# A hybrid decoder layer: projections in groups of 256 columns with one 512-column product for both parts of the moving operand

## The chip, the cores and the metric

The kernel runs on one core of a Trainium2 chip. The metric is the device time of one execution in microseconds (us), the median of several runs. TensorE (PE) multiplies: a weight load (LDWEIGHTS) brings in a stationary operand of up to 128 columns, and a product (MATMUL) streams a moving operand of up to 512 columns past it and adds the result in PSUM. VectorE (DVE), ScalarE (ACT) and GpSimd (POOL) do the elementwise work. Transfers are issued from the queue of SyncE (SP) in the main. Each engine executes its own instructions in program order, and semaphores order the engines among each other.

## What is computed

One decoder layer for 256 positions of width 2048 in float32: a normalisation, one large projection, two groups of attention heads, an output projection, and a mixture of 32 experts with two experts for each position. Cut to what matters:

```python
xn = rms_norm(h, attn_norm_w[layer])
proj = xn @ w_in[layer]                       # (256, 2048) @ (2048, 5696)
(nq, kcmp, vcmp, kslc, vslc, kwin, vwin, ngate, fq, fk, fv, ff) = jnp.split(proj, split_at, axis=-1)
o_nsa = nsa_mixer(...)                        # 16 heads, from the first eight
o_fox = fox_mixer(...)                        # 16 heads, from the last four
mixed = jnp.concatenate([rms_norm(o_nsa, nsa_out_norm_w[layer]),
                         rms_norm(o_fox, fox_out_norm_w[layer])], axis=-1)
h = h + mixed @ w_out[layer]
h = h + hier_moe(rms_norm(h, ffn_norm_w[layer]), ...)
return rms_norm(h, final_norm_w)
```

The change touches `xn @ w_in` alone. Its 64 columns for gates and forget logits are computed apart from the rest; 5632 columns remain.

## The kernel before

The projections are made with split operands. Every float32 matrix is written as a rounded part `hi` and a rest `lo`, both in a reduced float32 format, and a product of two such matrices is the sum of three products: hi with hi, hi with lo, lo with hi. They are added in the same place in PSUM.

x is transposed once at the start (`x_chunk`, L280): for each of 16 steps of depth (128 rows of the depth each) TensorE transposes two tiles, ScalarE writes the rounded part `xh(k)` and VectorE the rest `xl(k)`. They lie in four tiles `x0` to `x3` (L242): two for the rounded parts and two for the rests, eight steps each.

The weights are a stream of items (`items`, L161). An item is a tile of 1 MB, 512 rows by 512 columns, in one of three buffers `r0` to `r2` (`stream_dma`, L164). It is issued three items ahead. Each item is split in two halves by `stream_conv` (L179): ScalarE rounds 128x1024 elements, VectorE subtracts; the result goes to one of three buffers `c0` to `c2`, tiles named `cv_`. The split of a half is issued two halves ahead, and so waits until TensorE has read the half before the present one.

`project` (L306) makes four items for 512 columns, four steps of depth in each. A step (`chunk`) issues 12 products of 256 columns. For queries and keys ("T") the weights are stationary, in blocks of 128 columns, and x is the moving operand (`t_mm`, L289). For values ("N", half of the columns of a "TN" projection) x is stationary and the weights move (`n_mm`, L297). Each has its own weight load. The sums of a projection fill two PSUM banks, and four banks are there, so the next projection can run while the last is read out. There are 11 projections and 44 items: compressed keys and values (`kcv`), the keys and values of the two other branches (`kvs`, `kvw`), two of queries (`q`), and for the second head group two of queries (`fq`) and four of keys with values (`fkv`), where the two column ranges of 256 are loaded by two transfers.

After the last item of a projection `post` scales the sums by the row factors, straight out of PSUM: `row_scale` (L331) on VectorE, and for values a ScalarE scaling for each of two row tiles.

The first projection is written out on its own (L1036 to L1064), with the transposes and the sums of squares (`square`, L256) of x between its steps. From the second on, `run_items` (L225) issues after each step one step of `background`, four to an item: a stage of the attention of one pair of heads, and one step of the smaller work queued in `misc` and `splits`. Attention units are queued by `post` of the projection that completes their operands.

Behind the projections come the output projection (`out_block`, L884, tiles `wo`), 16 items whose products have 512 columns, with its operand split by `split_o` into the buffers `x0` to `x3` as these come free (`o_split`, L867); then the router; then 16 pairs of experts, whose weights come through a ring of buffers (`SLOTS`, L33) in a fixed order, each transfer issued when its buffer is released.

## Time and profile before

| | |
|---|---|
| median of 3 runs | 1419.55 us (1418.47 to 1419.59) |
| the profiled execution | 1417.83 us |
| its span | 1416.1 us |
| TensorE busy | 1310.2 us, 7462 products |
| VectorE, ScalarE busy | 496.6 us, 316.3 us |
| transfers | 480.02 MB |

The profile comes from one execution. Its page gives the busy time of each engine and its course over 40 slices; views of the trace give tables of stretches, the waits, the chain of work that ended last, and the instructions in order of time. Matmul durations in it overlap: one product is shown with some 280 ns where the next begins 120 ns later, so rates are read from the start of a run of products to its end, over their count.

### The profile page before, as it was taken

Reading aid. Unit: us, or ns where it says so; the run is one execution under the profiler, and the core shown is the slowest. Engines: PE = TensorE matmul, PEld = TensorE weight load, DVE = VectorE, ACT = ScalarE, POOL = GpSimd, SP = SyncE. Lnnn points to the kernel's source line nnn. Section 1 sums busy time; section 2 is a strip of 40 time slices with the busy share of each in tenths; the row PEclk is TensorE's granted clock in tenths of the full one; section 3 lists DMA queues with packets and bytes.
Section 4 is the critical chain, followed back from the end, with each engine's and each line's share of the span. In section 5 each row is a group of like instructions: output and inputs, shape, how many; then the busy total and the mean of one; then the engine's idle time right before and its main releaser. Section 6 shows DMA issues by size and latency. Waiting matters only on the chain.

```text
span 1416.1 us, 18174 instructions
## 1 busy us (share of the span) xinstructions
PE 1310.2 (93%) x7462; PEld 769.4 (54%) x7462; DVE 496.6 (35%) x990; ACT 316.3 (22%) x632; POOL 79.7 (6%) x95
## 2 busy tenths in 40 slices
PE   9999999999998999999988997997998899799885
PEld 8999899998787534334324333442433344243332
DVE  4656777767766204113103021220310212031022
ACT  5445555545544000000000000000010000000003
POOL 0300010221101003000000000000000000000003
PEclk9999999999999999999999999999999999999998
DMA  8654344654696899999999999999999999999994
GB/s 276 210 165 158 125 144 151 221 164 164 240 341 223 344 414 405 417 421 421 421 420 421 421 421 421 420 421 421 421 421 421 420 421 421 420 420 421 421 401 158
DMA packets 116697, 480.02 MB, mean 339 GB/s; under 512 B 14368, under 2 KB 40832, under 8 KB 68352
## 3 DMA queue, kind: packets, MB, share of 16 engines
q1 hardware_dynamic: 112240, 474.53, 84.6%
q10 hardware_dynamic: 4368, 4.27, 0.9%
q8 instruction: 60, 0.98, 0.3%
q14 instruction: 29, 0.24, 0.0%
HBM read 476.63 MB, written 2.14 MB: 338 GB/s over the span
## 4 chain that ended last, share of the span: by engine, by line
PE 50%; DMA 42%; DVE 4%; ACT 2%; issue 1%; POOL 0%; SPq 0%; DVEq 0%; ACTq 0%; POOLq 0%
DMA e_u<-in_expert_w_up_dram 16%; DMA e_d<-in_expert_w_down_dram 16%; DMA e_g<-in_expert_w_gate_dram 11%; PE bu L114 7%; PE fkv_ps L114 6%; PE wo L114 6%; PE bg L114 5%; PE by L114 5%; PE fq_ps L114 3%; PE bx L114 2%; PE q_ps L114 2%; PE bo L114 2%; PE kcv_ps L114 2%; PE kvw_ps L114 2%; PE kvs_ps L114 2%; PE o L114 2%
## 5 line engine op out<-in xcount | busy, mean ns | idle before, releaser
L114 PE MATMUL by<-e_d,hids 128*64 128x512 f32 (+2 forms) x1072 | 234.1, 576 | 32.3 <-DMA e_d<-in_expert_w_down_dram 31.7
L114 PE MATMUL bu<-e_u,xg 128*64 128x512 f32 x1024 | 242.5, 597 | 9.5 <-DMA e_u<-in_expert_w_up_dram 9.5
L114 PE MATMUL bg<-e_g,xg 128*64 128x512 f32 x1024 | 236.6, 596 | 12.5 <-DMA e_g<-in_expert_w_gate_dram 12.5
L1330 DVE TENSOR_TENSOR ys<-by,ys 128x512 fp32r<-128x512 f32 x60 | 40.0, 688 | 455.4 <-ACT ys L1329 454.3
L114 PEld LDWEIGHTS by<-e_d,hids 128*64 128x64 f32 x1072 | 78.4, 137 | 180.9 <-issue 121.2
L114 PEld LDWEIGHTS bg<-e_g,xg 128*64 128x64 f32 x1024 | 80.7, 137 | 145.7 <-issue 111.1
L114 PEld LDWEIGHTS bu<-e_u,xg 128*64 128x64 f32 x1024 | 78.6, 136 | 143.5 <-issue 114.3
L1344 DVE TENSOR_TENSOR y<-y,bo 128x512 f32<-128x512 f32 x112 | 72.0, 684 | 151.0 <-PE bo L114 151.0
L1329 ACT CAST ys<-by 128x512 fp32r<-128x512 f32 x60 | 35.2, 586 | 310.9 <-PE by L114 197.2
L114 PE MATMUL bo<-ys,scT 128*128 128x512 f32 x240 | 73.5, 427 | 13.3 <-DVE y L1344 5.8
L114 PE MATMUL wo<-cv_wo,ohi 128*128 128x512 f32 x256 | 80.6, 396 | 0.0
L114 PEld LDWEIGHTS bx<-s,hh 128*128 128x128 f32 x512 | 64.1, 193 | 23.7 <-issue 13.0
L114 PE MATMUL bx<-s,hh 128*128 128x256 f32 x512 | 70.4, 291 | 4.6 <-DVE y L1344 2.9
L114 PEld LDWEIGHTS bo<-ys,scT 128*128 128x128 f32 x240 | 38.0, 188 | 60.1 <-issue 45.1
L1258 DVE TENSOR_TENSOR xg<-bx,fw 128x512 f32<-128x512 f32 x64 | 43.6, 690 | 77.1 <-PE bx L114 77.1
L114 PE MATMUL fkv_ps<-xhl,cv_fkv 128*128 128x256 f32 x384 | 58.5, 288 | 0.0
L1452 POOL TENSOR_TENSOR o<-y,e_fnw 128x256 f32<-128x256 f32 (+2 forms) x12 | 10.1, 866 | 835.9 <-DVE y L1365 835.9
L114 PE MATMUL fkv_ps<-cv_fkv,xhl 128*128 128x256 f32 x384 | 56.4, 283 | 0.0
L114 PEld LDWEIGHTS wo<-cv_wo,ohi 128*128 128x128 f32 x256 | 46.9, 188 | 10.4 <-issue 1.2
L188 DVE TENSOR_TENSOR cv_fkv<-raw_fkv,cv_fkv 128x1024 fp32r<-128x1024 f32 x32 | 43.3, 1352 | 24.9 <-ACT cv_fkv L187 24.7
L114 PE MATMUL fq_ps<-xhl,cv_fq 128*128 128x256 f32 x384 | 51.6, 287 | 0.0
L114 PEld LDWEIGHTS fkv_ps<-xhl,cv_fkv 128*128 128x128 f32 x384 | 50.8, 191 | 1.3 <-issue 0.5
(288 smaller groups left out, 1397.3 us busy)
## 6 DMA issues: line engine op xcount, KB each, us to landing
e_g<-in_expert_w_gate_dram SPq DMA_DIRECT2D x128, 1024.0 KB, 19.8
e_u<-in_expert_w_up_dram SPq DMA_DIRECT2D x128, 1024.0 KB, 19.8
e_d<-in_expert_w_down_dram SPq DMA_DIRECT2D x124, 1024.0 KB, 19.8
raw_fkv<-in_w_in_dram SPq DMA_DIRECT2D x32, 512.0 KB, 4.5
raw_wo<-in_w_out_dram SPq DMA_DIRECT2D x16, 1024.0 KB, 5.5
raw_q<-in_w_in_dram SPq DMA_DIRECT2D x8, 1024.0 KB, 5.1
raw_fq<-in_w_in_dram SPq DMA_DIRECT2D x8, 1024.0 KB, 4.9
raw_kvs<-in_w_in_dram SPq DMA_DIRECT2D x4, 1024.0 KB, 6.9
```

The source lines that it names most:

```text
L114: pe.matmul(o, l, r, start=start, stop=stop, skip_group_check=True)
L188: dve.tensor_tensor(lo, r, hi.bitcast(F32), ALU.subtract)
L1258: dve.tensor_tensor(xt_[:, i0:i0 + per, 0:m], bx.rearrange("p (i s) -> p i s", i=per), fw[:, 4 * j + i0:4 * j + i0 + per].unsqueeze(2).bro ...
L1329: act.copy(hi, by[n])
L1330: dve.tensor_tensor(lo, by[n], hi.bitcast(F32), ALU.subtract)
L1344: dve.tensor_tensor(y[t][:, ns], base[t][:, ns], bo, ALU.add)
L1452: (dve if last else pool).tensor_tensor(o[t][:, ns], y[t][:, ns], fnw[:, ns], ALU.mult)
```

## The change

A projection is now 256 columns over the whole depth: two items of 1024 rows by 256 columns, with eight steps in each, and 22 projections of either kind "T" or "N". The two parts of an operand lie next to each other: `xb(k)` is `xh(k)` and `xl(k)` in 512 columns, and a split half of weights has `hi` and `lo` of a step side by side. One product of 512 columns multiplies the rounded stationary part with both parts of the moving operand at once; its result fills a whole bank, the product with hi in one half, that with lo in the other. A second product of 256 columns adds the stationary rest. At the end ScalarE copies one half out of PSUM, VectorE adds the other, and `post` reads the sum in SBUF. Half of the queries and of the compressed keys and values is so handed on two items earlier. Four background steps remain in each item. The x buffers change their order, and with them the ring. The first split of all is made in two parts.

```diff
-    psb = ps_st.enter_context(tc.tile_pool(name="psb", bufs=4, space=PSUM))
+    psb = ps_st.enter_context(tc.tile_pool(name="psb", bufs=2, space=PSUM))
...
+    def banks(name):
+        return psb.tile([P, 2, 512], F32, tag="b", name=name)
...
     def stream_conv(h):
...
-        cv = big.tile([P, 2, 2, 512], F32R, tag=f"c{h % 3}", name=f"cv_{nm}_{hf}")
-        hi, lo = cv[:, 0], cv[:, 1]
-        r = raws[i][:, 2 * hf:2 * hf + 2, :]
-        act.activation(hi, r, AF.Copy)
-        dve.tensor_tensor(lo, r, hi.bitcast(F32), ALU.subtract)
+        n2 = nk // 2
+        cv = big.tile([P, n2, 2, 2048 // nk], F32R, tag=f"c{h % 3}", name=f"cv_{nm}_{hf}")
+        hi, lo = cv[:, :, 0, :], cv[:, :, 1, :]
+        r = raws[i][:, n2 * hf:n2 * hf + n2, :]
+        n = n2 if h else n2 // 2
+        for k in range(0, n2, n):
+            act.activation(hi[:, k:k + n], r[:, k:k + n], AF.Copy)
+            dve.tensor_tensor(lo[:, k:k + n], r[:, k:k + n], hi[:, k:k + n].bitcast(F32), ALU.subtract)
...
-    xhl = [big.tile([P, 8, T], F32R, tag=f"x{i}", name=f"xhl{i}") for i in range(4)]
+    xhl = [big.tile([P, 4, 2, T], F32R, tag=f"x{i}", name=f"xhl{i}") for i in range(4)]
+
+    def xb(k):
+        return xhl[k // 4][:, k % 4].rearrange("p a t -> p (a t)")
...
-        mm(ps, hi[:, cs], xh(k), st, False)
-        mm(ps, hi[:, cs], xl(k), False, False)
-        mm(ps, lo[:, cs], xh(k), False, k == 15)
...
-        mm(ps, xh(k)[:, tk], hi[:, cs], st, False)
-        mm(ps, xh(k)[:, tk], lo[:, cs], False, False)
-        mm(ps, xl(k)[:, tk], hi[:, cs], False, k == 15)
...
+    def project(col, kind, name, post):
...
+        def chunk(kg, kk, hi, lo, both):
+            k = kg * 8 + kk
+            if not b:
+                b.append(banks(f"{name}_ps"))
+            for c in range(2):
+                cs = slice(c * P, c * P + P)
+                if kind == "T":
+                    mm(b[0][:, c, :], hi[:, cs], xb(k), k == 0, False)
+                    mm(b[0][:, c, 0:T], lo[:, cs], xh(k), False, k == 15)
+                else:
+                    mm(b[0][:, c, :], xh(k)[:, cs], both, k == 0, False)
+                    mm(b[0][:, c, 0:T], xl(k)[:, cs], hi, False, k == 15)
+
+        def end():
+            t_ = wk.tile([P, 2, T], F32, tag="sum", name=f"{name}_sum")
+            act.copy(t_, b[0][:, :, T:])
+            dve.tensor_tensor(t_, b[0][:, :, 0:T], t_, ALU.add)
+            post(t_)
+
+        for kg in range(2):
+            items.append((f"{name}{kg}", w_in[kg * 1024:(kg + 1) * 1024, col:col + 256], 8,
+                          lambda kk, hi, lo, both, kg=kg: chunk(kg, kk, hi, lo, both), end if kg == 1 else None))
...
-    project(C_KC, "T", "kcv", post_kcv)
-    project(C_KS, "TN", "kvs", lambda b: post_kv(b, 0))
-    project(C_KW, "TN", "kvw", lambda b: post_kv(b, 1))
+    for i in range(2):
+        project(C_KC + 256 * i, "T", f"kcv{i}", lambda s_, i=i: post_kcv(s_, i))
+    for br, col in enumerate((C_KS, C_KW)):
+        project(col + 256, "N", f"v{br}", lambda s_, br=br: post_v(s_, br))
+        project(col, "T", f"k{br}", lambda s_, br=br: post_k(s_, br))
...
+            project(C_FK + c, "T", f"fk{G}{hf}", kept.append)
+            project(C_FV + c, "N", f"fv{G}{hf}", lambda s_, G=G, hf=hf: post_fv(s_, G, hf))
...
-    for i in range(4):
-        _, _, chunk, post, _ = items[i]
+    for i in range(2):
+        post = items[i][4]
...
-        if i == n_proj - 3:
+        if i == n_proj - 2:
             o_split(0)
-            for q in range(8):
-                misc.append(split_later(q))
+            for q in range(0, 8, 2):
+                misc.append(split_later(q, q + 1))
             rs_o(0)
```

## Rows read from the trace of the kernel before

**Rows 1.** The page, parts 1 and 2: busy time; busy tenths in 40 slices.

```profile
PE 1310.2 (93%) x7462; PEld 769.4 (54%) x7462; DVE 496.6 (35%) x990; ACT 316.3 (22%) x632; POOL 79.7 (6%) x95
...
PE   9999999999998999999988997997998899799885
...
DMA  8654344654696899999999999999999999999994
```

**Rows 2.** Table of stretches: length, busy us by engine (instructions), clock, DMA share, GB/s.

```profile
37.77:99.40 61.63, 61.63 (x534) 58.99 (x533) 35.81 (x56) 25.39 (x32) 11.91 (x16) 1.00 0.55 174
99.40:157.50 58.10, 55.60 (x457) 53.85 (x456) 39.07 (x98) 32.81 (x66) 0.61 (x1) 1.00 0.50 163
157.50:194.60 37.10, 35.18 (x290) 33.16 (x289) 28.25 (x87) 22.18 (x54) 3.10 (x5) 1.00 0.40 129
194.60:259.70 65.10, 65.10 (x538) 61.83 (x538) 47.68 (x144) 36.66 (x94) 9.69 (x12) 1.00 0.50 151
259.70:348.40 88.70, 87.83 (x734) 82.64 (x734) 61.83 (x140) 45.30 (x98) 20.83 (x20) 1.00 0.56 185
348.40:447.70 99.30, 99.13 (x476) 79.23 (x475) 67.68 (x104) 50.17 (x78) 4.64 (x6) 1.00 0.69 254
520.00:600.00 80.00, 76.54 (x382) 31.89 (x380) 22.21 (x30) 6.84 (x14) 12.10 (x8) 1.00 1.00 412
```

**Rows 3.** TensorE's waits to 460 us: us in total, times, longest.

```profile
PE bpt L741 <- DVE st_n L641: 2.8, 2, 1.9
...
PE csc L114 <- DVE st_n L641: 1.0, 1, 1.0
PE o L114 <- DVE pT_f L607: 0.9, 1, 0.9
...
PE s_n L114 <- DVE q L695: 0.5, 1, 0.5
...
PE t_f L604 <- DVE st_f L588: 0.2, 1, 0.2
```

**Rows 4.** The same waits in the expert part, 520 to 1380 us.

```profile
PE by L114 <- DMA e_d<-in_expert_w_down_dram: 31.7, 24, 1.3
PE bg L114 <- DMA e_g<-in_expert_w_gate_dram: 12.5, 10, 1.3
PE bu L114 <- DMA e_u<-in_expert_w_up_dram: 9.5, 9, 1.3
```

**Rows 5.** The chain of work in order of time: start, us, what, count.

```profile
51.15 1.37 PE bgt L114 x12
...
99.41 20.17 PE q_ps L114 x168
...
376.80 35.49 PE wo L114 x156
...
575.40 13.73 PE by L114 x64
```

**Rows 6.** The page, part 5: busy us, mean ns of one, then idle before.

```profile
L1344 DVE TENSOR_TENSOR y<-y,bo 128x512 f32<-128x512 f32 x112 | 72.0, 684 | 151.0 <-PE bo L114 151.0
L1329 ACT CAST ys<-by 128x512 fp32r<-128x512 f32 x60 | 35.2, 586 | 310.9 <-PE by L114 197.2
```

**Rows 7.** Instructions in order of time at a projection's end: start, us, what [idle before].

```profile
318.26 0.68 DVE L336 TENSOR_TENSOR fox_m<-fkv_ps,rsb 128x512 f32<-128x512 f32 x1
...
318.91 0.84 ACT L797 ACTIVATE fox_m<-fkv_ps,rsx 128x256 f32<-128x256 f32 x2 [1.82 <-PE fkv_ps L114]
...
319.64 1.06 ACT L187 ACTIVATE cv_fkv<-raw_fkv 128x1024 fp32r<-128x1024 f32 x1
...
320.73 1.23 DVE L188 TENSOR_TENSOR cv_fkv<-raw_fkv,cv_fkv 128x1024 fp32r<-128x1024 f32 x1 [1.78 <-ACT cv_fkv L187]
```

**Rows 8.** The start: ScalarE and VectorE in order of time; last, a piece of the chain.

```profile
10.55 0.48 DVE L285 SCALAR_TENSOR_TENSOR xhl<-xt,vec,xhl 128x256 fp32r<-128x256 f32 x1
13.57 1.06 ACT L187 ACTIVATE cv_kcv<-raw_kcv 128x1024 fp32r<-128x1024 f32 x1 [1.28 <-DMA raw_kcv<-in_w_in_dram]
...
20.86 1.05 ACT L258 ACTIVATE oraw<-xs 128x1024 f32<-128x1024 f32 x1
21.80 0.19 ACT L258 ACTIVATION_READ_ACCUMULATOR oraw<-xs 128x1 f32 x1
22.14 0.47 ACT L284 ACTIVATE xhl<-xt,vec 128x256 fp32r<-128x256 f32 x1
...
32.02 5.76 PE kcv_ps L114 x48
```

**Rows 9.** Transfers: two groups of issues, one issue, and the gates' weights landing.

```profile
raw_fkv<-in_w_in_dram SPq DMA_DIRECT2D x32, 512.0 KB, 4.5
...
raw_q<-in_w_in_dram SPq DMA_DIRECT2D x8, 1024.0 KB, 5.1
...
14.65 7.43 SPq L376 DMA_DIRECT2D gmem<-in_w_in_dram  x1
...
DMA to landing us min/median/max: 2.9/7.3/10.7
```

More of the change, by code (lines that the diff above doesn't have):

```diff
@@ L226, in run_items @@
         for i in range(lo_i, hi_i):
-            _, _, chunk, post, _ = items[i]
+            nk, post = items[i][2], items[i][4]
             stream_dma(i + DMA_AHEAD)
-            for kk in range(4):
-                h = 2 * i + kk // 2
-                if kk % 2 == 0:
-                    stream_conv(h + 2)
-                hi, lo = halves[h]
-                chunk(kk, hi[:, kk % 2, :], lo[:, kk % 2, :])
-                background()
+            for kk in range(nk):
+                if kk % (nk // 2) == 0:
+                    stream_conv(2 * i + 2 + 2 * kk // nk)
+                run_chunk(i, kk)
+                if (kk + 1) % (nk // 4) == 0:
+                    background()
             if post is not None:
@@ L886, in out_block, with chunk @@
         ns = slice(n * 512, (n + 1) * 512)
-        def chunk(kg, kk, hi, lo):
+        def chunk(kg, kk, hi, lo, _):
             if not b:
-                b.extend(bank(f"wo{part}{n}{t}") for t in range(2))
+                bb = banks(f"wo{part}{n}")
+                b.extend(bb[:, t, :] for t in range(2))
             k = part * 8 + kg * 4 + kk
@@ L912, in out_block @@
             r0 = part * 1024 + kg * 512
[L913 to L914 removed]
+            items.append((f"wo{part}{n}{kg}", w_out[r0:r0 + 512, ns], 4,
+                          lambda kk, hi, lo, both, kg=kg: chunk(kg, kk, hi, lo, both), post if kg == 1 else None))
     for part in range(2):
@@ L1034, in tile_kernel @@
     stream_dma(2)
-    for i in range(4):
-        _, _, chunk, post, _ = items[i]
+    for i in range(2):
+        post = items[i][4]
         if i:
             stream_dma(i + DMA_AHEAD)
-        for kk in range(4):
-            k = 4 * i + kk
+        for kk in range(8):
+            k = 8 * i + kk
             if k == 0:
```

166 lines of the change are left out of this document (74 added, 92 removed).

## The prediction

> **What bounds the kernel now.** I read the page first, then the stretches, then what TensorE waits for, then the chain. The page shows TensorE busy for most of the span and the DMA engines full only from about the 17th of 40 slices on [rows 1]. The table of stretches cuts the first third: in the projections (up to 348.4 us) and the output projection (to 447.7 us) the PE column is nearly the whole length of each stretch, VectorE stands at 58% to 76%, ScalarE at 41% to 60% and the DMA share at 0.40 to 0.69; from 520 us on the DMA share is 1.00 [rows 2]. So the front part is bound by TensorE's instruction stream and the expert part by transfers. TensorE's waits in the projection part after the first 40 us come to 2.8 + 1.0 + 0.9 + 0.5 + 0.2 = 5.4 us, all on VectorE [rows 3]. In the expert part it waits for expert weights, 31.7 + 12.5 + 9.5 us [rows 4]. That transfer stream has a fixed number of bytes behind a start that the program places after the output projection: what the front part gains or loses moves the end by as much.
>
> **What a product costs.** Where nothing else interrupts, 168 products of 256 columns take 20.17 us, 120.1 ns each, and 156 of 512 columns take 35.49 us, 227.5 ns each [rows 5]. The granted clock of these stretches is 1.00 in the table [rows 2], the 2.4 GHz level, at which 256 and 512 columns last 106.7 and 213.3 ns: each product thus shows some 13 to 14 ns over its columns, whatever its length. Both rows have a new 128-column stationary operand for each product.
>
> **The change, part by part.**
>
> *Products.* 5632 columns are projected (the gates' 64 go another way): 44 blocks of 128 by 16 steps of depth, 704 groups. (For the values, two blocks of 128 rows by 22 blocks of 256 columns: 704 as well.) Each group now has three 256-column products, 2112 in all; it will have one of 512 and one of 256. Three cost 3 x 120.1 = 360.3 ns, the pair 227.5 + 120.1 = 347.6 ns: 12.7 ns less, and 704 x 12.7 ns = 8.9 us. The columns are the same, 768: what goes is one fixed part per group, not a third of the work. No stretch of before has 512 and 256 in turn. From below the pair could cost 360 ns (the 512-column product pays the fixed part twice), which saves nothing. From above the nearest rows have 64-column weights: 64 products of 512 columns in 13.73 us (214.5 ns) and 12 of 256 in 1.37 us (114.2 ns) [rows 5], a pair of 328.7 ns, so 31.6 ns and 22 us saved. I take 12.7 ns: the two rows with 128-column weights are the nearest, and they agree on the fixed part.
>
> The Trainium skill, "TensorE: Matmul & The Clock Gate", section "Back-to-back issue gap", gives the isolated warm gap as N/2.4 + 2.5 ns, as an estimate 109.2 and 215.8 ns here, and speaks against most of this gain: a group would save 2.5 ns and all of them 1.8 us. The trace disagrees with its size: the measured 120.1 and 227.5 ns have a fixed part five times as large.
>
> *The halves' sum.* Each of the 22 new projections of 256 columns ends with a ScalarE copy of 128x512 out of PSUM and a VectorE addition of the same size, then the old scaling. By the nearest rows these take 0.586 us (L1329) and 0.684 us (L1344) [rows 6], 12.9 us on ScalarE and 15.0 us on VectorE. Neither engine sets the end in a mean: in the busiest stretch VectorE has 28.25 of 37.1 us [rows 2], and one addition in two items (some 16 us there) brings 76% to 80%. What can hurt is the order on ScalarE. The copy waits for the last product, and the split of the next weights (`stream_conv`, ScalarE then VectorE, 1.06 + 1.23 us) is queued behind it; so for the values are two ScalarE scalings (0.84 us), which now wait for VectorE's addition [rows 7]. At the end of a value projection the chain is 0.59 + 0.69 + 0.84 + 1.06 + 1.23 = 4.4 us, where it was 3.1. The half made ready is read two halves later, 2 x 8 x 347.6 ns = 5.6 us. So 1.2 us are left without attention work in between, more where attention products stretch the halves; but there VectorE has its own queue. I price these meetings at 1.0 us in all. Lower end: -0.5 us, since half of q is split two items earlier, which may remove the 0.5 us wait on q [rows 3]. Upper end: one addition in front of each of the five occurrences of the other VectorE waits there, 5 x 0.69 = 3.5 us.
>
> *The start.* x is transposed and split (`x_chunk`, ScalarE 0.47, VectorE 0.48 us) step by step beside the first projection. Before, a step held 12 products; now it holds 4, and all of x is wanted within the first 256 columns. ScalarE is held until 13.57 us by a DMA, then has before the last x_chunk: 12 of these (5.6 us), three splits (3.2 us) and three squares of 1.05 + 0.19 us (3.7 us) [rows 8], 12.5 us less about 0.1 us of overlap at each of 18, so until some 24.5 us. The last products of the first 256 columns then end near 27 us, and the second 256 columns add 32 x 347.6 ns = 11.1 us: 38.1 us, where these 512 columns now end at 32.02 + 5.76 = 37.8 us [rows 8]. So the saving of the first 64 groups (0.8 us) is not seen and 0.4 us is lost on top, +1.2 us against the sum. Lower end 0, if TensorE stays the bound; upper end 2.2 us, if weights in rows of 1 KB rather than 2 KB land about 1 us later (an estimate: 1 MB in 2 KB rows lands in 5.1 us, 512 KB in 1 KB rows in 4.5 us [rows 9]).
>
> *Moved, at no cost.* There are still 44 items of 1 MB and four background steps each, so attention units come at the same items. Gates and compression begin some five steps earlier, the first reader of the gates' weights some 32 us after the start; the longest of their loads is issued from 14.65 us for 7.43 us [rows 9] and lands within 10.7 us [rows 9]. The output split (`o_split`) starts one item later, and its first operand is ready within item 43 while the output projection starts with item 44. PSUM has the same four banks, as two pairs; a pair is read at once after its projection and wanted a whole projection, 11 us, later. For each of these the cover is some microseconds of products; without it, its one DMA landing or 0.9 us split would show.
>
> *Sum.* -8.9 + 1.0 + 1.2 = -6.7 us. The profiled execution took 1417.83 us, of which 1416.1 us are the span: 1411.1 us. The median of before lies 1.7 us above that execution; against it the forecast is 1419.55 - 6.7 = 1412.9 us. Its own ends: -8.9 - 0.5 + 0 = -9.4 and -8.9 + 3.5 + 2.2 = -3.2 us, so 1410.1 to 1416.4 us. A difference under 0.2% (2.8 us) can't be told from none here.
>
> **The rivals.**
>
> *Slower: the split of the weights falls behind.* If VectorE's backlog at the end of a projection passes the 1.2 us left, each of the 22 ends stalls TensorE by the excess. With 0.55 us at each of the 22, 12 us are lost instead of 1.0: 1424 us; from 0.35 us at each nothing is gained, and from 0.48 us it is slower by what can be measured. For it: VectorE is 76% busy in one stretch and waits there already end on it. Against it: 75% is no backlog, and the products of the attention units lengthen the very halves in which VectorE is loaded.
>
> *No gain: a 512 beside a 256 saves no fixed part.* The pair costs 360 ns; 1.0 + 0.4 us remain: 1421 us. For it, only that no row shows the mixture; against it, both rows of 128-column weights. By the gap of the Trainium skill (the section above) it would be, as an estimate, some 1419 us, with 1.8 us saved.
>
> *Bursts eat half.* The start and the sums both cost about twice their price, without the systematic backlog: -8.9 + 2.0 + 2.4 = -4.5 to -8.9 + 3.5 + 4.4 = -1.0 us, 1415 to 1418.6 us.
>
> *More: weight loading hides entirely* behind the 512-column products, the far bound of 22 us less the same costs: -20 us, 1400 us. For it: 256-column products leave loading little cover. Against it: the 512-column row has twice the cover and the same fixed part.
>
> **How the numbers follow.** Forecast 0.68; bursts 0.12; slower 0.08; no gain 0.07; more 0.05. The range takes the forecast's ends, a microsecond below for the pair's cost, and the bursts: 1409 to 1419 us; slower, no gain and more (0.20) are left out. Faster by over 0.2%: 0.68 + 0.05 + a third of the bursts = 0.77; within: the other bursts and no gain, 0.15; slower: 0.08.
>
> **What would show it.** In the profile after, an undisturbed stretch of a projection should have four pairs in some 1.39 us, where twelve products took 1.44; weight loads in the projections should fall from 2112 to 1408. TensorE's waits for `cv_` tiles should stay near zero after 40 us; if they don't, the slower rival is at work. The first value products should begin near 38 us. The output projection should begin some 6 to 7 us earlier than 348.4 us, and the first wait for expert weights be moved by the same amount; if the end moves by less than the output projection does, the transfers' start isn't tied to it as I hold. A pair at 360 or 329 ns makes the forecast wrong at its first term.

## The result and the profile after

The change made the kernel slower. The median of four executions is 1427.51 us (1425.63 to 1428.26), beside 1419.01 us (1418.40 to 1419.59) for the kernel before on the same chip: 1.0058 of it, with an interval of 1.0041 to 1.0075, some 8 us more. The prediction was 1412.9 us.

The profiled execution took 1426.94 us, of which 1425.0 us are the span (before: 1416.1 us). Page, part 1: busy time, share of the span, instructions.

```profile
PE 1305.2 (92%) x6758; PEld 733.7 (51%) x6758; DVE 510.8 (36%) x1013; ACT 328.3 (23%) x655; POOL 80.0 (6%) x95
```

Beside [rows 1] there are 704 products and 704 weight loads fewer, as planned, and TensorE is busy 5 us less in a span that is 9 us longer. So it waits more. The table of stretches follows, with stage borders of its own: the first value product, the first query product, the first of the second head group, and in the output projection the first and the last product with `ohi`, the rounded part of its operand (0.2 to 0.3 us before the last product of all; "its last product" below is this one). The columns are those of [rows 2].

```profile
42.40:103.40 61.00, 60.37 (x403) 51.37 (x402) 37.02 (x54) 27.00 (x36) 9.36 (x9) 1.00 0.58 174
103.40:166.20 62.80, 55.77 (x330) 48.21 (x329) 43.12 (x104) 36.06 (x71) 0.61 (x1) 0.95 0.50 151
166.20:356.00 189.80, 185.04 (x1175) 155.96 (x1174) 140.32 (x377) 108.69 (x255) 33.12 (x37) 1.00 0.53 163
356.00:456.40 100.40, 98.48 (x472) 79.01 (x471) 68.52 (x106) 50.85 (x80) 4.64 (x6) 1.00 0.70 251
```

Against the kernel before, whose borders by the same products lie at 37.6, 99.3, 157.5, 348.4 and 447.1 us (within 0.6 us of those of [rows 2]), the start is 4.8 us longer (42.4 for 37.6), values and keys 0.7 us shorter (61.0 for 61.7), the query stage 4.6 us longer (62.8 for 58.2), the second head group 1.1 us shorter (189.8 for 190.9) and the output projection 1.7 us longer (100.4 for 98.7). The output projection begins at 356.0 instead of 348.4 us and its last product at 456.4 instead of 447.1: 9.3 us, and the span's end moves by 8.9 us. What comes behind the output projection adds nothing to that, and TensorE's waits for expert weights between 500 and 1380 us are about the same: 31.8 + 12.7 + 11.4 us, where they were 31.7 + 12.5 + 9.5 us [rows 4].

TensorE's waits from 20 to 460 us (the waits view: total, times, longest), to be laid beside [rows 3]:

```profile
PE bpt L744 <- DVE st_n L644: 7.7, 2, 6.5
PE o L116 <- ACT pT_n L671: 1.8, 2, 1.0
PE s_f L116 <- DVE fox_m L337: 1.7, 2, 1.1
PE o L116 <- DVE pT_f L610: 1.0, 1, 1.0
PE t_f L607 <- DVE st_f L591: 0.8, 1, 0.8
...
PE q_ps L116 <- DVE cv_q L191: 0.5, 1, 0.5
```

Waits for the split of the weights (`cv_`), the place at which the slower rival of the prediction looked, come to 0.5 us. All the larger ones are in the attention: a score bank (`bpt` takes the bank that VectorE's L644 frees), the transposed probabilities, the scaled keys of the second group.

**The query stage.** VectorE's and ScalarE's instructions in order of time where the 6.5 us arise (start, us, instruction, idle before and its releaser):

```profile
145.21 1.22 DVE L191 TENSOR_TENSOR cv_q<-raw_q,cv_q 128x1024 fp32r<-128x1024 f32 x1
146.34 0.68 DVE L322 TENSOR_TENSOR q_sum<-q_ps,q_sum 128x512 f32<-128x512 f32 x1
147.06 0.69 DVE L339 SCALAR_TENSOR_TENSOR scaled<-q_sum,rsb 128x512 f32<-128x512 f32 x1
147.84 0.62 ACT L692 CAST q<-scaled 64x512 fp32r<-64x512 f32 x1 [4.01 <-DVE scaled L339]
148.48 0.61 ACT L696 CAST q<-scaled 64x512 fp32r<-64x512 f32 x1
148.49 0.68 DVE L693 TENSOR_TENSOR q<-scaled,q 64x512 fp32r<-64x512 f32 x1 [0.74 <-ACT q L692]
...
149.78 0.69 DVE L698 TENSOR_TENSOR q<-scaled,q 64x512 fp32r<-64x512 f32 x1 [0.60 <-ACT q L697]
150.86 1.22 DVE L191 TENSOR_TENSOR cv_q<-raw_q,cv_q 128x1024 fp32r<-128x1024 f32 x1 [0.39 <-ACT cv_q L190]
152.00 0.42 DVE L644 CUSTOM_DVE_ANT_0 pr_n<-s_n,bias 128x256 f32<-128x256 f32 x1
...
152.91 0.66 PE L744 MATMUL bpt<-cst,pcm 128*128 128x128 f32 x2 [6.49 <-DVE st_n L644]
```

The scores that L644 reads were ready by 144.6 us. In front of it in VectorE's queue now stand the addition of the halves, the scaling and the two rests of the first half of a query projection, with two waits on ScalarE in between, and only then the split of weights and L644. That block is the part of `post_q` which the change moved from the end of the second half to the end of the first. TensorE, in program order, does nothing until 152.91 us. What follows is slow too (columns as above; the first stretch is the last 3.9 us of the wait):

```profile
149.00:152.90 3.90, 0.00 (x0) 0.01 (x1) 2.91 (x8) 2.21 (x5) 0.00 (x0) 0.50 0.97 322
152.90:156.00 3.10, 3.08 (x11) 2.75 (x12) 1.89 (x11) 3.10 (x11) 0.00 (x0) 0.56 0.02 5
```

The granted clock is at its 1.2 GHz level at the end of the wait and stays there for most of the next 3 us.

**The start.** The two stretches of the first 22.5 us in which products run, and ScalarE's queue there:

```profile
10.00:16.00 6.00, 2.97 (x18) 2.16 (x16) 3.04 (x5) 3.57 (x6) 0.00 (x0) 0.97 1.07 375
16.00:22.50 6.50, 6.05 (x22) 5.38 (x23) 3.76 (x7) 3.62 (x7) 0.00 (x0) 0.50 1.12 337
```

```profile
10.71 1.06 ACT L190 ACTIVATE cv_kcv<-raw_kcv 128x1024 fp32r<-128x1024 f32 x1 [1.35 <-DMA raw_kcv<-in_w_in_dram]
...
13.68 1.06 ACT L190 ACTIVATE cv_kcv<-raw_kcv 128x1024 fp32r<-128x1024 f32 x1 [1.55 <-DMA raw_kcv<-in_w_in_dram]
14.64 1.19 ACT L295 ACTIVATE xhl<-xt,vec 128x256 fp32r<-128x256 f32 x3
17.17 0.47 ACT L295 ACTIVATE xhl<-xt,vec 128x256 fp32r<-128x256 f32 x1 [1.34 <-PE xt L294]
...
22.30 0.47 ACT L295 ACTIVATE xhl<-xt,vec 128x256 fp32r<-128x256 f32 x1 [1.23 <-PE xt L294]
...
28.03 0.48 ACT L295 ACTIVATE xhl<-xt,vec 128x256 fp32r<-128x256 f32 x1
```

To 16 us TensorE starves (2.97 of 6.00 us busy), because the parts of x wait in ScalarE's queue behind two splits that wait for transfers. From 16 us the clock is at the 1.2 GHz level, and now ScalarE waits for TensorE's transposes (1.34 and 1.23 us). The last part of x is made at 28.03 us; the forecast had some 24.5. In all, ScalarE waits 3.7 us for transposes from 16 to 28 us.

### The profile page after: what moved, and what is told of

Its sections match the earlier page's. It is cut to its first block, busy times and chain, and to the rows that moved or that the text cites. A ratio compares the mean times of both kernels' runs of the same rounds, so it can differ in the third digit from the quotient of the medians.

```text
span 1425.0 us, 16784 instructions
## 1 busy us (share of the span) xinstructions
PE 1305.2 (92%) x6758; PEld 733.7 (51%) x6758; DVE 510.8 (36%) x1013; ACT 328.3 (23%) x655; POOL 80.0 (6%) x95
## 3 DMA queue, kind: packets, MB, share of 16 engines
q10 hardware_dynamic: 4368, 4.27, 0.9%
## 4 chain that ended last, share of the span: by engine, by line
PE 50%; DMA 36%; DVE 7%; ACT 4%; issue 2%; SPq 0%; ACTq 0%; POOL 0%; DVEq 0%; POOLq 0%
DMA e_u<-in_expert_w_up_dram 14%; DMA e_d<-in_expert_w_down_dram 14%; PE bu L116 11%; DMA e_g<-in_expert_w_gate_dram 7%; PE bg L116 6%; PE wo L116 6%; PE by L116 6%; PE bo L116 3%; PE bx L116 2%; PE fq_ps L116 2%; PE fv_ps L116 2%; PE q_ps L116 2%; PE o L116 2%; PE v_ps L116 2%; PE fk_ps L116 2%
## 5 line engine op out<-in xcount | busy, mean ns | idle before, releaser
L116 PE MATMUL by<-e_d,hids 128*64 128x512 f32 (+2 forms) x1072 | 236.1, 576 | 32.5 <-DMA e_d<-in_expert_w_down_dram 31.8
L116 PE MATMUL bu<-e_u,xg 128*64 128x512 f32 x1024 | 242.4, 597 | 11.4 <-DMA e_u<-in_expert_w_up_dram 11.4
L116 PE MATMUL bg<-e_g,xg 128*64 128x512 f32 x1024 | 234.7, 596 | 12.7 <-DMA e_g<-in_expert_w_gate_dram 12.7
L1289 ACT CAST scT<-bsc 128x256 fp32r<-128x256 f32 x16 | 6.0, 372 | 193.8 <-PE bsc L116 193.8
L116 PE MATMUL fq_ps<-xhl,cv_fq 128*128 128x512 f32 (+1 forms) x256 | 50.5, 344 | 0.0
L1326 ACT COPY hids<-bh 128x512 f32<-128x512 f32 x16 | 9.4, 586 | 178.1 <-PE bh L1324 178.1
L116 PE MATMUL wo<-cv_wo,olo 128*128 128x512 f32 x128 | 50.0, 390 | 0.0
L1315 ACT ACTIVATE hids<-bg,c 128x512 f32<-128x512 f32 x16 | 11.0, 688 | 169.0 <-PE bg L116 169.0
```

Source lines behind the costliest of these rows:

```text
L116: pe.matmul(o, l, r, start=start, stop=stop, skip_group_check=True)
L1289: act.copy(scT, bt[:, :T])
L1315: act.activation(hids[-1], bg_, AF.Silu, scale=c2[:, 1:2])
L1326: act.copy(hT, bh.rearrange("p (i s) -> p i s", i=4))
```

## The experiments

First products of the stages, read from the tile view of each kernel's trace (us; the kernels are explained below). The last column is the time against the kernel before on the same chip, with its 95% interval. The times are medians of four to eight executions, but the starts of a row come from one profiled execution each. Executions of one kernel on one chip lie up to 4.7 us apart (the kernel before: 1416.33 to 1421.02 us), and the profiled one of "three products, one half" took 1423.50 us where its median is 1425.70 us. So a difference of a microsecond or so between two rows shows nothing by itself.

| kernel | values | queries | 2nd group | output proj. | its last product | ratio |
|---|---|---|---|---|---|---|
| before | 37.6 | 99.3 | 157.5 | 348.4 | 447.1 | 1 |
| changed | 42.4 | 103.4 | 166.2 | 356.0 | 456.4 | 1.0058 (1.0041 to 1.0075) |
| three products, one half | 42.5 | 103.7 | 165.5 | 354.4 | 453.8 | 1.0053 (1.0033 to 1.0073) |
| three products, two halves | 42.0 | 103.9 | 167.9 | 359.6 | 460.0 | 1.0094 (1.0077 to 1.0111) |
| without additions | 40.8 | 101.0 | 162.3 | 348.7 | 448.1 | – |
| by length | 41.6 | 102.3 | 166.1 | 355.5 | 456.0 | 1.0050 (1.0034 to 1.0065) |
| clock held at the start | 39.8 | 100.8 | 164.9 | 354.8 | 455.3 | 1.0058 (1.0041 to 1.0075) |
| first 512 together | 39.0 | 102.1 | 166.4 | 356.5 | 456.9 | 1.0069 (1.0053 to 1.0086) |
| the same, loads later | 36.1 | 96.6 | 161.0 | 350.8 | 451.3 | 1.0029 (1.0018 to 1.0039) |
| queries late | 42.8 | 103.7 | 163.9 | 356.8 | 457.3 | 1.0075 (1.0058 to 1.0091) |
| queries spread | 41.7 | 102.7 | 161.1 | 352.4 | 452.8 | 1.0053 (1.0036 to 1.0069) |
| values fused | 42.5 | 102.5 | 165.8 | 353.0 | 452.6 | 1.0040 (1.0026 to 1.0054) |
| three repairs | 36.1 | 96.7 | 153.7 | 342.0 | 441.7 | 0.9959 (0.9945 to 0.9972) |
| three repairs, by length | 36.4 | 96.8 | 155.0 | 343.0 | 442.7 | 0.9962 (0.9948 to 0.9976) |

### What a pair costs: three products of 256 columns instead of it

```diff
-                    mm(b[0][:, c, :], hi[:, cs], xb(k), k == 0, False)
+                    mm(b[0][:, c, 0:T], hi[:, cs], xh(k), k == 0, False)
+                    mm(b[0][:, c, T:], hi[:, cs], xl(k), False, False)
```

(For the values likewise.)

> One part undone: three products of 256 columns in place of the pair, all else as in the change. By the rates in the trace of the change (32 pairs in 11.31 us, 353.4 ns, against 360.3 ns for three) 704 groups cost 4.9 us more: 1431 to 1433.5 us. By the forecast's 12.7 ns a group: 8.9 us more, 1435.5 to 1437 us. If the pair saves nothing in place: 1427 to 1428 us.

It took 1431.24 us, 1.0094: the pair saves 0.36% of the time, 5.1 us (by the two intervals together, some 2 to 8 us), and 3.6 us up to the output projection. The chain of work that ended last has the longest stretches of products; here in the changed kernel, then with three products.

```profile
103.58 11.32 PE q_ps L116 x64
...
163.60 2.78 PE q_ps L116 x16
```

```profile
104.04 11.53 PE q_ps L116 x96
...
165.22 2.87 PE q_ps L116 x24
```

32 undisturbed groups take 11.32 / 32 = 353.8 ns with the pair and 11.53 / 32 = 360.3 ns with three, 6.5 ns apart where 12.7 were forecast. Another 32 groups, of values (`fv_ps`), show the same: 11.31 and 11.53 us. In some short stretches between attention units the pair does take 2.78 / 8 = 347.5 ns, the value of the sum, and three take 358.8 ns. So the gain per group lies between 6.5 and 11.3 ns, 4.6 to 7.9 us for all 704.

### Is it the alternation of lengths: the two 512s of a step first

```diff
             for c in range(2):
...
                     mm(b[0][:, c, :], hi[:, cs], xb(k), k == 0, False)
-                    mm(b[0][:, c, 0:T], lo[:, cs], xh(k), False, k == 15)
...
+            for c in range(2):
...
+                    mm(b[0][:, c, 0:T], lo[:, cs], xh(k), False, k == 15)
```

> The changed kernel, but the two products of 512 columns of a step are issued first and its two products of 256 columns after them, so that the length changes every second product instead of at each one. 32 pairs take 353.4 ns each where they alternate; the single lengths' rows of the kernel before gave 347.6 ns. Theory A: a change of length costs 3 ns each time. Then a pair takes 350.5 ns, 2.0 us are saved over all projections, and the output projection begins near 354 us instead of 356.0 us. Theory B: the pair has its price whatever the order, the 512-column product with both parts of an operand pays more than the row of the output projection. Then 32 pairs take 352.5 to 354.5 ns each, and the time is that of the changed kernel, 1.0058 of the kernel before within 0.0015.

```profile
102.47 11.16 PE q_ps L116 x64
```

11.16 / 32 = 348.8 ns: the undisturbed pair gets 5.0 ns cheaper, a little more than theory A's 3 ns, and theory B falls for the pair. So the fixed part of [rows 5] nearly holds for products among their like (347.6 ns by the sum), and in undisturbed stretches the alternation adds 5 ns a pair. The 2.0 us that theory A gave for the output projection did not come: it begins 0.5 us earlier, and the time can't be told from that of the changed kernel (1.0050 against 1.0058). Some short stretches had the low price already; whether that is the whole reason is not shown. With the three repairs (at the end) the order changed nothing either.

### What the additions cost

First the changed kernel without them:

```diff
             act.copy(t_, b[0][:, :, T:])
-            dve.tensor_tensor(t_, b[0][:, :, 0:T], t_, ALU.add)
             post(t_)
```

> Leaves out VectorE's addition of the second half at the end of each projection (22 of 128x512; the sums lack their main part), with ScalarE's copy kept. If the additions cost TensorE's stream about what I priced for all the sums (1.0 us) or less: 1426 to 1427.5 us. If the queue order around them is what the slower rival said: 3 us or more less, under 1424.5 us.

The output projection begins at 348.7 us instead of 356.0. The whole time (5042.67 us) says nothing on the change: the altered sums send other numbers of positions to the experts, and a loop for overfull experts runs. Of the 7.3 us, 1.6 lie before the first value product, where at most two additions stand; among the runs of the table that have one and the same start, it varies from 41.7 to 42.8 us. So a second run was made that leaves the sums right: three products, all added into one half of the bank. Its edit, against the kernel with three products in two halves (for the values likewise):

```diff
-                    mm(b[0][:, c, T:], hi[:, cs], xl(k), False, False)
+                    mm(b[0][:, c, 0:T], hi[:, cs], xl(k), False, False)
...
-            act.copy(t_, b[0][:, :, T:])
-            dve.tensor_tensor(t_, b[0][:, :, 0:T], t_, ALU.add)
+            act.copy(t_, b[0][:, :, 0:T])
```

> The changed kernel's groups of 256 columns over the whole depth with the three products of 256 columns as before the change, all added into one half of the bank: no halves to add, so ScalarE's copy stands alone and VectorE's 22 additions are gone; the result is the reference's. It differs by the additions alone from the run with three products in two halves (1.0094 of the kernel before, the output projection from 359.6 us). Theory A: the additions cost the front part about 7.3 us, as the run without them showed, whose own end couldn't be compared. Then the output projection begins at 351.5 to 353.5 us and the time is 1.0035 to 1.0050 of the kernel before: grouping alone, with its start and its earlier split of the queries, still loses 5 to 7 us. Theory B: in that run the altered numbers, not the missing additions, made the difference. Then the output projection begins at 358 us or later and the time is 1.0080 or more.

It took 1425.70 us. Beside the run with two halves the additions alone cost 1.0094 - 1.0053 = 0.41%, 5.8 us (by the two intervals together, some 2 to 9 us). In the two profiles it is 5.2 us up to the output projection (0.7 in values and keys, 2.2 in the queries, 2.8 in the second head group, -0.5 at the start) and 1.0 us within it. Theory A held, at 354.4 us a little behind its figure. TensorE's larger waits, with two halves and then with one, show where the additions arrive:

```profile
PE bpt L746 <- DVE st_n L646: 7.3, 2, 6.1
PE s_f L116 <- DVE fox_m L339: 1.6, 2, 1.0
PE o L116 <- ACT pT_n L673: 1.2, 2, 0.8
```

```profile
PE bpt L745 <- DVE st_n L645: 5.4, 2, 5.1
...
PE s_f L116 <- DVE fox_m L338: 0.4, 1, 0.4
```

The wait for the probabilities is gone without them, and that for the scaled keys nearly so. The long wait for the score bank is not: 5.1 us are left, so an addition in front of L644 lengthens it by about 1 us and does not make it.

The same run says what the regrouping costs without pair and additions: 6.0 us at the output projection (+4.9 at the start, -0.5 in values and keys, +3.6 in the queries, -2.0 in the second group), 0.53% of the time. ScalarE's 22 copies are in that figure, and so are the other rearrangements (the order of the x buffers, the first split in two parts, the output split one item later); no run parts them.

### How an addition reaches TensorE: values scaled and added without a copy

The end of a value projection in the changed kernel, ScalarE and VectorE:

```profile
233.94 0.59 ACT L321 COPY fv_sum<-fv_ps 128x512 f32<-128x512 f32 x1 [0.57 <-PE fv_ps L116]
...
235.82 0.91 ACT L806 ACTIVATE fox_m<-fv_sum,rsx 128x256 f32<-128x256 f32 x2 [1.29 <-DVE fv_sum L322]
236.64 1.04 ACT L190 ACTIVATE cv_fk<-raw_fk 128x1024 fp32r<-128x1024 f32 x1
237.71 1.22 DVE L191 TENSOR_TENSOR cv_fk<-raw_fk,cv_fk 128x1024 fp32r<-128x1024 f32 x1 [1.33 <-ACT cv_fk L190]
...
238.85 0.42 DVE L644 CUSTOM_DVE_ANT_0 pr_n<-s_n,bias 128x256 f32<-128x256 f32 x1
...
241.91 1.30 PE L116 MATMUL o<-pT_n,vN 128*64 128x256 f32 x12 [1.03 <-ACT pT_n L671]
```

ScalarE waits for VectorE's addition (1.29 us), VectorE then for ScalarE's split (1.33 us), the scores behind it start late, and TensorE waits at the end of that chain for the probabilities. The edit takes ScalarE's wait away:

```diff
+    def scale_sum(dst, ps):
+        for t in range(2):
+            act.activation(dst[:, t, :], ps[:, t, T:], AF.Copy, scale=rsx[:, t:t + 1])
+        for t in range(2):
+            dve.scalar_tensor_tensor(dst[:, t, :], ps[:, t, 0:T], rsx[:, t:t + 1], dst[:, t, :], ALU.mult, ALU.add)
```

> The changed kernel, but for the six value projections ScalarE scales one half straight out of PSUM and VectorE scales and adds the other half in one instruction for each row tile: no copy of the sum, and ScalarE no longer waits for VectorE's addition before the next split and the attention's copies behind it. Without any addition (the experiment that left them out) the stretch from the second head group's first product to the output projection took 186.3 us instead of 189.8. Theory A: most of that is ScalarE's queue held at the value projections' ends (1.29 us there at each). Then the stretch takes 187 to 188 us and the time is 1424.5 to 1426 us. Theory B: it is the additions' length on VectorE. VectorE's work is then as long as before (two instructions of 0.48 us for one of 0.69), the stretch stays at 189.5 to 190.5 us and the time at 1427 to 1428.5 us.

```profile
233.56 0.84 ACT L550 ACTIVATE fox_m<-fv_ps,rsx 128x256 f32<-128x256 f32 x2 [0.58 <-PE fv_ps L116]
234.29 1.06 ACT L190 ACTIVATE cv_fk<-raw_fk 128x1024 fp32r<-128x1024 f32 x1
```

The split comes 0.7 us behind the scaling's start instead of 2.7 us behind the copy's. The waits for `pT_n` are gone, the second head group takes 187.2 us instead of 189.8, the output projection begins at 353.0 us, and the time is 1423.34 us. VectorE's work there is no shorter (0.87 us for 0.68), so it is what stands in ScalarE's queue, theory A. The copy (0.59 us) left that queue together with the wait (1.29 us), and the run does not part the two. The six value projections give back 3.0 us at the output projection; in the time alone the gain is within the intervals (1.0040 against 1.0058). The sixteen others (queries and keys) still have their copy and addition.

### The first half of the queries: put back, or spread

Put back to the end of the second half, where it was before the change:

```diff
-        evac_q(s_, q, i)
...
-            qs2[G] = m8(f"m{2 + G}", f"q{G}", (4, 2, T), F32R)
-            split_q(q, qs2[G], 0)
+            kept.append(s_)
...
+        evac_q(kept.pop(), q, 0)
+        split_q(q, qs, 0)
+        evac_q(s_, q, 1)
```

> One part undone: the sum of the first half of each query projection is kept, and its scaling and split are done together with those of the second half, as in the kernel before. Theory A (the split of q1's first half, moved into the stretch in which VectorE also has the compressed scores and the first attention unit, makes TensorE wait 6.5 us for a score bank, and the clock then falls): the wait of bpt falls from 7.7 us to 2 to 4 us, no stretch at the lower clock near 150 us, time 1420 to 1422.5 us (5 to 7 us less than the 1427.5 of the change). Rival B (the copy and the addition of the halves are what holds VectorE and ScalarE, wherever the split stands): the wait stays over 5 us, time 1426 to 1428 us.

TensorE's waits from 60 to 200 us:

```profile
PE bpt L744 <- DVE st_n L644: 2.4, 2, 1.3
PE s_n L116 <- DVE q L693: 2.0, 1, 2.0
PE csc L116 <- DVE st_n L644: 1.8, 1, 1.8
```

The long wait is gone, as theory A said, and the query stage 2.6 us shorter, but the time is 1428.84 us, no less, and a little above rival B's figure. The block is the same, only later and twice as long, and now scores wait for q itself (2.0 us) and the clock falls there instead (0.72 from 171 to 177 us). The theory that the early split alone was the loss fell: undone by itself, it gives nothing back. Neither place is good for this block of dependent instructions. The third way is to cut it up, between the attention's steps:

```diff
-        evac_q(s_, q, i)
...
+    def split_q_first(s_, q, G):
+        evac_q(s_, q, 0)
+        yield
+        qs2[G] = m8(f"m{2 + G}", f"q{G}", (4, 2, T), F32R)
+        split_q(q, qs2[G], 0)
+        yield
...
+            misc.append(split_q_first(s_, q, G))
```

> The changed kernel, but the evacuation, scaling and split of the first half of a query projection are handed to the background queue as two steps between the attention's steps, instead of being issued in one piece at the projection's end. In the changed kernel TensorE waits there 6.5 us for a score bank that VectorE frees behind this piece, and the clock is 0.50 to 0.56 for the 7 us after it. Theory A: what hurts is the one piece in front of the score bank, and the clock after the wait. Then the wait for the bank is below 3 us, the second head group's products begin at 161 to 163 us instead of 166.2, the clock is 1.00 from 149 to 156 us, and the time is 1422 to 1424.5 us. Theory B: the queues of VectorE and ScalarE are short of time as a whole, so that a stall taken away here comes back in the next stage, as it did when the split was put back to its old place (1428.8 us). Then the output projection begins at 355.5 us or later all the same, and the time is 1426.5 us or more.

The wait for the bank falls from 6.5 to 2.6 us, the second head group begins at 161.1 us instead of 166.2, and the output projection at 352.4 us: theory A for these. The addition and a split of weights still stand in front of L644 there, and the clock is still low for a while (0.62 from 148 to 152 us), against what A said. (The 7 us of low clock that the expectation gives to the changed kernel are the last 3.9 us of the wait and the 3.1 us behind it.) The time, 1425.09 us, lies between the theories. At 1.0053 (interval 1.0036 to 1.0069) its gain is smaller than at the output projection, and from this run alone it couldn't be told from none; 0.7 of the 3.6 us at the output projection were there at the first value product already, before the edit does anything.

### The start: the clock, the pace, the transfers

Products that nobody reads, to keep TensorE busy while it waits for x:

```diff
+            if k in (3, 4):
+                keep_clock(f"hold{k}", 7)
```

> The changed kernel, with seven products of 128 columns, whose result nobody reads, put in front of the transposes of x for the 4th and the 5th step of the start, where TensorE otherwise waits for the split of x. In the changed kernel TensorE starves there from about 10 to 16 us, and the granted clock is 0.50 from 16 to 22.5 us; the values' first products begin at 42.4 us where 38.1 us were forecast. Theory A: more than half of those 4.3 us come from the lower clock. Then the clock stays at 1.00 in that stretch, the values begin at 39 to 40 us, the output projection 2 to 3 us earlier than at 356.0 us, and the time is 1424.5 to 1425.5 us. Theory B: the pace at which ScalarE and VectorE hand over x sets the start. Then the values begin at 41.5 to 43 us with a clock of 1.00 too, and the time stays at 1427 to 1428.5 us.

```profile
10.00:16.00 6.00, 5.65 (x44) 5.20 (x44) 2.77 (x4) 3.57 (x6) 0.00 (x0) 1.00 1.07 375
16.00:22.50 6.50, 6.22 (x42) 5.50 (x42) 4.79 (x10) 5.27 (x11) 0.00 (x0) 1.00 1.14 331
```

With the clock at 1.00 the last part of x is made at 25.42 instead of 28.03 us, and the values begin at 39.8 instead of 42.4 us: 2.6 of the 4.3 us by which the forecast of the start was missed (42.4 against 38.1 us) are the clock. The other 1.7 us are put down to the pace, as the remainder. Of the 2.6 us half is lost again in the query stage (64.1 instead of 62.8 us), the output projection begins 1.2 us earlier, and the time is that of the changed kernel (1.0058 for both). Theory A held for the start, B for the time.

The other way is to need x more slowly, with the first 512 columns projected together:

```diff
+    def project_pair(col, name, posts):
...
+            for c in range(4):
+                cs = slice(c * P, c * P + P)
+                mm(b[c // 2][:, c % 2, :], hi[:, cs], xb(k), k == 0, False)
+                mm(b[c // 2][:, c % 2, 0:T], lo[:, cs], xh(k), False, k == 15)
```

> One part undone: the first two projections of 256 columns run together, step by step, on weights in items of 512 rows by 512 columns, with the pair of products kept. Theory A (with 4 products in a step instead of 12, the transposes and splits of x can't keep up, TensorE starves from 10 to 16 us and its clock falls to the lower level from 16 to 22.5 us): the first value product at 37 to 38 us instead of 42.4, time 1422 to 1424 us. Rival B (what delays the start is the sums, or the load on the transfers, not the pace): first value product after 40 us, time 1425.5 to 1428 us.

```profile
34.03 1.06 ACT L190 ACTIVATE cv_v<-raw_v 128x1024 fp32r<-128x1024 f32 x1 [4.27 <-DMA raw_v<-in_w_in_dram]
...
36.98 1.05 ACT L346 COPY kcv_sum<-kcv_ps 128x512 f32<-128x512 f32 x2
```

The values began at 39.0 us, between the theories. The products themselves were done by 34.5 us. But all four banks were in use, and the copies that free them stood in ScalarE's queue behind a split that waited 4.27 us for its weights; TensorE waited 4.2 us, the clock was 0.57 for the next 7 us, and by the output projection the gain was gone (356.5 us). So the same projection once more, with the loads of the gates' weights and the like behind the values' first weights:

```diff
+        if i == 2:
+            early_loads()
...
-                early_loads()
```

> The changed kernel, but the first 512 columns are projected together, as before the change: 512 rows by 512 columns an item, 16 steps of 8 products, in all four banks; and the loads of the gates' weights and the like are issued one item later, so that the values' first weights don't queue behind them. When only the first was done, the first projection's products ended by 34.5 us instead of about 42, but TensorE then waited 4.2 us for the banks, because ScalarE stood waiting for the values' weights until 34.0 us and read the banks out after that; the clock was 0.57 for the 7 us behind. Theory A: the late transfer is the cause of that wait. Then the values begin at 35.5 to 37 us, the clock is 1.00 behind it, and the output projection begins 3 to 5 us earlier than at 356.0 us: 1422.5 to 1424.5 us. Theory B: with all four banks in use the read-out itself (two copies, two additions, 2.5 us) is what TensorE waits for. Then the values begin at 37.5 us or later and the time is 1425.5 to 1428 us.

Theory A. In the run without this the issue of one of the gates' loads (`gmem`) holds SyncE's queue for 8.53 us from 14.08 us on, and the values' first weights are issued at 28.36 us; now it is 17.75 us. The values begin at 36.1 us, 1.5 us earlier than before the change, the wait for the banks is 0.7 us, the clock is 1.00 from 6 to 60 us, the gain of 5.2 us stands at the output projection (350.8 us), and the time is 1421.68 us.

### Together

> The changed kernel with three of the repairs together: the first 512 columns projected together and the later loads moved (alone it brought the output projection from 356.0 to 350.8 us), the values scaled and added without a copy (353.0 us), and the first half of the queries handed to the background queue (352.4 us). Theory A: these losses lie in different stages and each is paid on its own, so their repairs add: 5.2 + 3.0 + 3.6 = 11.8 us, the output projection begins at 343.5 to 345.5 us, before its 348.4 us in the kernel before, and the ends as in the single runs (1422.0 - 5.4 - 2.8 - 2.1 of span) give 1415 to 1418 us, 0.998 to 1.0005 of the kernel before. Theory B: the queues of VectorE and ScalarE are short as a whole, and what one repair gives the next stage takes. Then the output projection begins at 347 us or later and the time is 1.001 to 1.003 of the kernel before.

The last repair of each kind (loads later, queries spread, values fused) in one kernel: 1413.39 us, beside 1418.65 us for the kernel before on the same chip, 0.9959 with an interval of 0.9945 to 0.9972. With the next one it is the fastest of all, and beats the kernel before by 5 us. The output projection begins at 342.0 us, 14.0 us earlier than in the changed kernel, where the single repairs add up to 11.8 us. So the losses lie in different stages, theory A; both this start and the time are better than the figures of theory A, and why the repairs together give more than their sum is not shown. Nor did any run give the kernel before what the repairs contain besides (the later loads, the queries in steps), so how much of the 5 us is the merit of the pair is open. What TensorE still waits for from 20 to 460 us, the three largest but for the router's wait, which is as before:

```profile
PE bpt L776 <- DVE st_n L676: 4.5, 2, 2.7
...
PE s_f L116 <- DVE fox_m L364: 2.3, 2, 1.3
PE bx L116 <- DVE s L1179: 1.0, 1, 1.0
```

> The three repairs together, and the products of a step in the order of their length (the 512-column ones first, then the 256-column ones). By theory A of the run on the order (3 ns for each change of length) the output projection begins 2 us earlier than with the three repairs alone, at 341.5 to 343.5 us, and the time is 0.9965 to 0.9990 of the kernel before. By theory B the order changes nothing: the same as the three repairs alone within 0.7 us at the output projection's start and within 0.1% in the time.

1413.40 us, 0.9962, the output projection at 343.0 us. That start is 1.0 us later than without the order, a little more than theory B allowed, and the time is the same: the order of the products changes nothing that can be measured here.

## Why the prediction was wrong

Three steps of the table lead from the kernel before to the changed one: before to one half, one half to two halves, two halves to changed. So the 7.6 us by which the output projection comes later are a sum: regrouping with its copies +6.0, additions +5.2, pair -3.6. The forecast had +1.2 (the start), +1.0 (the sums, copies included), -8.9. All three terms erred, and all to one side: 4.8, 4.2 and 5.3 us, the 14.3 us between a forecast of 6.7 us less and 7.6 us more. What failed in the first two is one step: the waits of ScalarE and VectorE for each other and for TensorE were priced where the trace of before showed them or where the next split of weights stands, and not in the queues that the edit makes.

*Products, -8.9 forecast.* Right in kind, about half in size: 6.5 ns a group in undisturbed stretches, times 704 = 4.6 us; by the run with three products 3.6 us up to the output projection and 5.1 us in the time. The step that failed is that the rows with one length alone were carried over to a mixture of lengths, which had no row. The bound from below (360 ns) covered it, but the range kept -8.9 us at both of its ends. The estimate by the Trainium skill's isolated gap ("TensorE: Matmul & The Clock Gate", section "Back-to-back issue gap"), 1.8 us saved, is too low: the measured pair, 353.8 ns, is neither the 325 ns that this estimate gives nor 347.6.

*The halves' sums, +1.0 forecast, at most 3.5.* Measured 5.2 us at the output projection and 1.0 us behind it. The upper end took the waits that were in the trace of before and put one addition in front of each. But waits came where there had been none: the probabilities (`pT_n`) 1.8 us, the scaled keys (`fox_m`) 1.7 us. By the run with one half they are mostly the additions' doing. The text had the mechanism in hand (two scalings that "now wait for VectorE's addition", with ScalarE's queue behind them) and followed it to the split of weights alone, where it found 1.2 us left. The next weights were in time; what was late next was the attention's own work behind the split, in the same two queues. In the same way the slower rival had the right kind of cause and the wrong place: `cv_` waits stayed at 0.5 us.

*The start, +1.2 forecast, at most 2.2.* Of the 1.2 us, 0.8 were a saving of the pair that was not to be seen there, so the values were to begin 0.4 us later than before; they began 4.8 us later. Adding up ScalarE's instructions gave the last part of x at 24.5 us; it came at 28.03. The sum assumed that ScalarE is never idle after 13.57 us. It was, for 3.7 us, waiting for transposes, and for the most part because TensorE had starved before and ran at the 1.2 GHz level: with the clock held it waits 1.2 us. Against the forecast's 38.1 us, 2.6 us are the clock and the remaining 1.7 us are put down to the pace.

*Moved, at no cost.* This part counted buffers and loads; the earlier split of half of q stands in the forecast only as a possible gain of 0.5 us, at the lower end of the sums. It didn't list the queue that the split was moved into: with the addition seven instructions on two engines, three of which wait for the other engine, in front of a score bank that TensorE wants. There is the largest single wait of the projections, 6.5 us (5.1 us without an addition), and the lower clock behind it. Without pair and additions the query stage is 3.6 us longer than before. The move alone is not shown to be a net loss, since putting the block back gained nothing in the changed kernel; cutting it up gained some 3 us.

*What held.* TensorE's instruction stream bounds the front part, and what it loses moves the end by as much: 9.3 us at the last product of the output projection, 8.9 us of span. The weight loads fell by 704. That with the three repairs the output projection begins 6.4 us earlier than before, within the 6 to 7 us that were forecast, is chance: the pair saves less than its term, and the repaired start alone brings the values 1.5 us earlier than before, which no term held. One reading was wrong without effect: the DMA row of [rows 1] is full from the 15th slice on, not the 17th.

What stays open: why short stretches take 347.5 ns a pair without the reordering; what ScalarE's 22 copies and the other rearrangements cost by themselves; and how the price of the additions divides among queries, keys and values.

## What to carry to other kernels

When an edit adds small work to engines that are off the critical path, list the queue at each place where it is put, instruction by instruction, up to the next result that TensorE wants, and price the wait of each one that depends on the other engine; the busy shares of 58% to 76% said nothing on that here, and the waits of the old trace were no bound. A block of dependent instructions that is moved should be cut into steps between the other work, not put down whole somewhere else. And an engine's idle microseconds have to be priced with what the clock does after them.

## What the runs showed of the hardware

*Gaps cost more than their length.* After TensorE had stood still for 6.5 us, the granted clock was 0.50 at the end of the gap and 0.56 over the next 3.1 us; after a stretch at half load (2.97 of 6.00 us busy) it was 0.50 for 6.5 us. Held busy with useless products, the same start ran at 1.00 and was 2.6 us shorter. The Trainium skill ("TensorE: Matmul & The Clock Gate", section "HAM oscillation — how this bites in real kernels") describes the same for a kernel that waits for transfers again and again: after each wait the products run at the lower clock. The trace agrees, and shows it for waits on another engine as well.

*Length in turn costs.* A 512-column product with a 256-column one in turn takes 353.8 ns in undisturbed stretches, in order of length 348.8 ns, both with new 128-column weights for each product. In short stretches between attention units the alternating pair shows 347.5 ns as well.
